# A hybrid encoder step: down-weight differences nine steps behind their fetches, their stores fourteen

## The chip, the cores and the metric

The kernel runs on one core of one Trainium2 chip, in one launch. The metric is the device time in microseconds, the median of several runs. TensorE is PE below, VectorE DVE, ScalarE ACT, GpSimd POOL; SP is the engine whose queue issues most transfers.

## The reference, cut to what matters

One layer, width 1024, float32, over a prompt of 2048 rows and a sample of 8 x 16 rows:

```python
h = rms_norm(x); z = h @ w_in
A = chunk_band_attention(z)            # 8 heads x 64, own chunk of 64 + 8 before, relative bias
B = mlstm(z)                           # 4 heads x 128, exp input gate, running-max stabiliser
x = x + rms_norm(concat(rms_norm(A), sigmoid(o) * head_rms_norm(B)) @ w_out)
u = rms_norm(x) @ w_up                 # 2 x 2816 columns
y = causal_conv_width_3(u)
x = x + rms_norm((gelu(gate) * up) @ w_down)
```

What the change touches is `w_down` alone. The kernel multiplies by it with fast products in which blocks of `w_down` are combined beforehand by subtraction; those combinations are called differences here, and they depend on the weights only.

## The kernel before, in words

Until about 1000 us of the span the kernel is in its mixers. The input projection runs as 14 groups of columns (`GROUPS`: va, qk, qb, vo) for each of two halves of the rows. Every float32 product is made as three passes over a high and a low part (`mm3`, lines 100 to 102), so each weight tile `wi{i}_raw` is split by ACT (`wi_h`) and DVE (`wi_l`). Beside each unit of the projection `pump` takes steps of two pipes, one of attention heads (`s`, `tmp`, `mn`, `pt`) and one of mLSTM heads (masks `mb`, decay weights `w`, `ms`, `ma`, `num`, state `cst`), by a budget of PE and DVE costs. The sample's attention reads cached keys (`skr`) and values (`svr`) and a bias (`nbs`). The projection's results leave through staging tiles (`qk_st`) to DRAM and are fetched again by the heads (`qraw`, `kraw`, `vraw`). Then come the output projection and the conv FFN in three blocks of rows.

The FFN needs four differences of `w_down`'s blocks. The generator `folds` makes them ahead, during the mixers, in 22 pieces (11 row groups `k`, two column halves `c`). A piece is a fetch of 128x4x256 floats (512 KB) by SP into one of three buffers, four subtracts of 128x256 on DVE in place (line 1182), and a store by SP to `wtd[k]` in DRAM (line 1202). `next(fold)` takes one step of it in each unit of the groups 2 to 12, and the rest runs out at the end of the last group. `FOLD_STEPS` is 12, so a new piece is fetched every 12 steps. In the code before, the subtracts are emitted 3 steps behind the fetch and the store 5 steps behind it. `wtd` is first read in the FFN, at 1733 us.

The whole program is recorded first. A scheduler with a model of the engines then sets each engine's order, from the recorded order, the dependences and its own times; the fetches and stores of the pieces are kept in program order among themselves. So the number of steps says where a piece is recorded, not where it runs. A transfer on SP or ACT is counted on one of eight completion counters in turn, and an issue waits for the earlier transfer on its counter.

Of the kernel before, what the change touches and what calls it, by code (L numbers as in the profile page):

```python
# [10 lines left out]
F32 = mybir.dt.float32  # L11
F32R = mybir.dt.float32r
AF = mybir.ActivationFunctionType
ALU = mybir.AluOpType
# [3 lines left out]
P = 128  # L18
D = 1024
# [21 lines left out]
NK = NF // 2  # L41
FOLD_STEPS = 12
# [7 lines left out]
def hymba_step(ctx: ExitStack, tc: tile.TileContext, I: dict, O: dict):  # L50
    nc = tc.nc
# [7 lines left out]
    def ps_mm(name):  # L59
        return psum.tile([P, 512], F32, tag="mm", name=name)  # L60

    def ps_big(name):
        return psum.tile([P, 1024], F32, tag="big", name=name)

    def ps_sm(name):
        return psum.tile([P, 512], F32, tag="sm", name=name)

    def dt_(shape, name):
        return dram.tile(shape, F32, tag=name, name=name)
# [51 lines left out]
    wtd = [dt_([P, 2048], f"wtd{k}") for k in range(NK)]  # L121
# [12 lines left out]
    pr = p1.enter_context(tc.tile_pool(name="pr", bufs=1))  # L134
# [1024 lines left out]
            nc.scalar.copy(hi, lo.bitcast(F32))  # L1159
            nc.vector.tensor_tensor(lo, lo.bitcast(F32), hi, op=ALU.subtract)  # L1160

    def fold_pieces():

        for k in range(NK):
            for c in range(2):
                yield f"d{k}_{c}", I["w_down"][k], wtd[k], c, True

    def folds():

        v4 = lambda t: t.rearrange("p (a n) -> p a n", a=4)  # L1170
        live = deque()
        pieces = list(fold_pieces())

        def load(nm, src, dst, c, down):
            cols = slice(c * 256, (c + 1) * 256)
            t = v4(pr.tile([P, D], F32, tag="fold", name=f"fold{nm}", bufs=3))
            tc.keep_in_program_order(nc.sync.dma_start(t, v4(src)[:, :, cols]))
            live.append((t, v4(dst)[:, :, cols], down))

        def combine(t, dst, down):  # L1180
            a, b, c, d = [t[:, i] for i in range(4)]
            sub = lambda o, x, y: nc.vector.tensor_tensor(o, x, y, op=ALU.subtract)
            if down:
                sub(a, b, a)
                sub(b, c, b)
                sub(c, c, a)
                sub(d, d, c)
            else:
                sub(a, a, d)
                nc.vector.tensor_tensor(d, d, c, op=ALU.add)  # L1190
                sub(c, c, a)
                sub(b, b, c)

        for n in range(FOLD_STEPS * (len(pieces) + 1)):
            i, r = divmod(n, FOLD_STEPS)
            if r == 0 and i < len(pieces):
                load(*pieces[i])
            if (n - 3) % FOLD_STEPS == 0 and 0 <= n - 3 < FOLD_STEPS * len(pieces):
                combine(*live[-1])
            if (n - 5) % FOLD_STEPS == 0 and 0 <= n - 5 < FOLD_STEPS * len(pieces):  # L1200
                t, dst, _ = live.popleft()
                tc.keep_in_program_order(nc.sync.dma_start(dst, t))
            yield

    GROUPS = ["va0", "qk0", "qk1", "va1", "qk2", "qk3", "qb0", "vo0", "qb1", "vo1", "qb2", "vo2", "qb3", "vo3"]
# [39 lines left out]
    norms = norm_steps(0)  # L1245
    next(norms)
    fold = folds()
    pend = load_group(0)
    for _ in pend[2]:
# [3 lines left out]
    for n_, (half, gi) in enumerate(seq):  # L1253
        wh, wl, _ = pend
# [5 lines left out]
        i = int(g[2])  # L1260
        nm = f"{g}_{half}"
# [208 lines left out]
    for b, tiles in enumerate(FBLOCKS):  # L1470
        last = b == len(FBLOCKS) - 1
        nt = len(tiles)
        n = HALF[b]
# [120 lines left out]
        for fi, f in enumerate(FORDER):  # L1594
# [8 lines left out]
            nm = f"{b}_{f}"  # L1603
            a, d_, ec = ps_mm(f"ua{nm}"), ps_sm(f"ub{nm}"), ps_big(f"uec{nm}")
            e, c = ec[:, 0:512], ec[:, 512:1024]
# [46 lines left out]
        if not last:  # L1652
# [47 lines left out]
            for p, (_, _, set_, onto) in enumerate(SEQUENCE):  # L1700
                for c in range(3):
# [8 lines left out]
                    for k in range(4 * c, min(4 * c + 4, NK)):  # L1710
                        i = 6 * p + k // 2
# [189 lines left out]
```

## Time and profile before

| | us |
|---|---|
| median of 3 runs | 2814.16 (2811.02 to 2815.5) |
| the profiled execution, whole | 2809.64 |
| its span | 2807.9 |
| PE busy in the span | 2707.0 |
| DVE busy | 1971.0 |
| ACT busy | 1441.0 |
| fetches of pieces: first and last start | 67.4 and 870.2 |
| stores of pieces: first and last start | 88.0 and 913.0 |

The span runs from the first to the last recorded instruction; the execution takes 1.74 us more. Busy time of engines overlaps, so it does not add up. The clock granted to PE was 0.992 of the full one over the span.

### The profile page before, as it was taken

Reading aid. Unit: us, or ns where it says so; the run is one execution under the profiler, and the core shown is the slowest. Engines: PE = TensorE matmul, PEld = TensorE weight load, DVE = VectorE, ACT = ScalarE, POOL = GpSimd, SP = SyncE. Lnnn points to the kernel's source line nnn. Section 1 sums busy time; section 2 is a strip of 40 time slices with the busy share of each in tenths; the row PEclk is TensorE's granted clock in tenths of the full one; section 3 lists DMA queues with packets and bytes.
Section 4 is the critical chain, followed back from the end, with each engine's and each line's share of the span. In section 5 each row is a group of like instructions: output and inputs, shape, how many; then the busy total and the mean of one; then the engine's idle time right before and its main releaser. Section 6 shows DMA issues by size and latency. Waiting matters only on the chain. (4 is left out here: it accounts for less than half of the span.)

```text
span 2807.9 us, 47466 instructions
## 1 busy us (share of the span) xinstructions
PE 2707.0 (96%) x16389; PEld 2524.4 (90%) x16389; DVE 1971.0 (70%) x3685; ACT 1441.0 (51%) x2922; POOL 474.9 (17%) x895
## 2 busy tenths in 40 slices
PE   8899999999899999999999999999999999999998
PEld 7899999988799997888899997789999778999877
DVE  5355555656556667767899998668888885888855
ACT  4354444635346666543454547555455565555533
POOL 1000010212100002235222211111111221222220
PEclk9999999999999999999999999999999999999999
DMA  5645456567574555345655557675555797555585
GB/s 187 178 131 159 149 173 189 174 195 236 171 223 146 159 158 173 127 147 183 232 185 170 194 173 263 201 242 163 174 176 162 273 309 240 173 177 178 184 311 185
DMA packets 359888, 535.12 MB, mean 191 GB/s; under 512 B 58882, under 2 KB 198110, under 8 KB 359518
## 3 DMA queue, kind: packets, MB, share of 16 engines
q1 hardware_dynamic: 319134, 491.95, 55.2%
q10 hardware_dynamic: 38592, 33.83, 3.6%
q0 software_dynamic: 1920, 6.29, 0.6%
q8 instruction: 129, 2.11, 0.3%
q14 instruction: 113, 0.93, 0.1%
HBM read 383.87 MB, written 151.21 MB: 191 GB/s over the span
## 5 line engine op out<-in xcount | busy, mean ns | idle before, releaser
L100 PE MATMUL uec<-B,wuh 128*128 128x384 f32 (+1 forms) x720 | 236.7, 330 | 10.8 <-DVE uu L1633 7.4
L101 PE MATMUL uec<-B,wuh 128*128 128x384 f32 (+1 forms) x720 | 235.5, 327 | 0.0
L102 PE MATMUL uec<-B,wul 128*128 128x384 f32 (+1 forms) x720 | 234.2, 327 | 0.0
L1322 ACT CAST wuh<-wu 128x512 fp32r<-128x512 f32 x255 | 141.8, 618 | 84.1 <-PE uec L101 79.5
L1323 DVE TENSOR_TENSOR wul<-wu,wuh 128x512 fp32r<-128x512 f32 x255 | 165.3, 685 | 15.3 <-ACT wuh L1322 11.7
L100 PE MATMUL vo<-wi_h,hT 128*128 128x256 f32 x544 | 157.4, 289 | 2.3 <-DVE mt L207 2.3
L102 PE MATMUL vo<-wi_h,hT 128*128 128x256 f32 x544 | 156.7, 288 | 0.0
L101 PE MATMUL vo<-wi_l,hT 128*128 128x256 f32 x544 | 156.4, 288 | 0.0
L100 PEld LDWEIGHTS uec<-B,wuh 128*128 128x128 f32 x720 | 135.4, 188 | 16.7 <-DVE uu L1633 10.0
L1323 DVE TENSOR_TENSOR wdl<-wdr,wdh 128x512 fp32r<-128x512 f32 x198 | 130.1, 700 | 27.1 <-ACT wdh L1322 27.1
L401 DVE CUSTOM_DVE_ANT_0 tmp<-s,nb 128x640 f32<-128x640 f32 (+4 forms) x128 | 94.2, 737 | 73.3 <-PE s L391 72.8
L402 ACT ACTIVATE tmp<-tmp,mn 128x640 f32<-128x640 f32 (+4 forms) x128 | 97.7, 763 | 84.1 <-DVE mn L401 82.8
L100 PE MATMUL qk<-hT,wi_h 128*128 128x384 f32 (+1 forms) x384 | 130.1, 339 | 7.8 <-ACT qk_st L234 4.3
L101 PEld LDWEIGHTS uec<-B,wuh 128*128 128x128 f32 x720 | 135.6, 188 | 0.2
L102 PEld LDWEIGHTS uec<-B,wul 128*128 128x128 f32 x720 | 135.4, 188 | 0.0
L1322 ACT CAST wdh<-wdr 128x512 fp32r<-128x512 f32 x198 | 111.7, 617 | 44.0 <-DMA wdr<-in_w_down 16.7
L414 DVE TENSOR_TENSOR ptl<-pt,pth 128x640 fp32r<-128x640 f32 (+4 forms) x128 | 93.8, 737 | 54.2 <-ACT pth L413 53.5
L102 PE MATMUL qk<-hT,wi_l 128*128 128x384 f32 (+1 forms) x384 | 129.9, 338 | 0.0
L100 PE MATMUL dn<-wdh,ah 128*128 128x512 f32 x308 | 122.8, 399 | 6.8 <-ACT wdh L1322 6.2
L101 PE MATMUL qk<-hT,wi_h 128*128 128x384 f32 (+1 forms) x384 | 128.7, 335 | 0.0
L101 PE MATMUL qb<-hT,wi_h 128*128 128x384 f32 (+1 forms) x384 | 128.3, 334 | 0.0
L100 PE MATMUL qb<-hT,wi_h 128*128 128x384 f32 (+1 forms) x384 | 127.6, 332 | 0.0
(445 smaller groups left out, 9144.8 us busy)
## 6 DMA issues: line engine op xcount, KB each, us to landing
wu<-in_w_up SPq DMA_DIRECT2D x220, 256.0 KB, 4.0
wu<-wsd SPq DMA_DIRECT2D x176, 256.0 KB, 3.9
wdr<-in_w_down SPq DMA_DIRECT2D x110, 256.0 KB, 5.4
wi_raw<-in_w_in SPq DMA_DIRECT2D x52, 512.0 KB, 4.5
wsd<-ws SPq DMA_DIRECT2D x88, 256.0 KB, 2.5
wdr<-wtd SPq DMA_DIRECT2D x88, 256.0 KB, 6.0
ad_S<-g SPq DMA_DIRECT2D x88, 192.0 KB, 2.0
ar<-ad_S SPq DMA_DIRECT2D x40, 384.0 KB, 4.8
```

The source lines that it names most:

```text
L100: nc.tensor.matmul(out, ah, bh, start=start, stop=False, skip_group_check=onto)
L101: nc.tensor.matmul(out, ah, bl, start=False, stop=False, skip_group_check=onto)
L102: nc.tensor.matmul(out, al, bh, start=False, stop=stop, skip_group_check=onto)
L401: nc.vector.tensor_tensor_reduce(o_, s_, b_, 1.0, 3e38, ALU.add, ALU.min, accum_out=mn)
L402: nc.scalar.activation(tmp[:, :n], tmp[:, :n], AF.Exp, bias=mn, scale=-1.0, accum_out=rsum[:, i % 4, hh:hh + 1])
L414: nc.vector.tensor_tensor(s.ptl[:, sl, qc], ptv, s.pth[:, sl, qc], op=ALU.subtract)
L1322: nc.scalar.copy(h, r)
L1323: nc.vector.tensor_tensor(l, r, h, op=ALU.subtract)
```

## The change

The subtracts of a piece are recorded nine steps behind its fetch instead of three, and its store five steps behind that, 14 steps behind the fetch instead of five; with 12 steps between fetches a store is now recorded after the next piece's fetch. A branch for another kind of piece, which was never taken, and the generator that listed the pieces are gone, and the tile is named `fold` instead of `foldd`. The subtracts are now on line 1176, the stores on line 1180, and every later line has a number that is 16 lower.

```diff
...
-        for n in range(FOLD_STEPS * (len(pieces) + 1)):
-            i, r = divmod(n, FOLD_STEPS)
-            if r == 0 and i < len(pieces):
-                load(*pieces[i])
-            if (n - 3) % FOLD_STEPS == 0 and 0 <= n - 3 < FOLD_STEPS * len(pieces):
-                combine(*live[-1])
-            if (n - 5) % FOLD_STEPS == 0 and 0 <= n - 5 < FOLD_STEPS * len(pieces):
-                t, dst, _ = live.popleft()
-                tc.keep_in_program_order(nc.sync.dma_start(dst, t))
...
+        def load(i):
+            k, c = pieces[i]
+            live[i] = v4(pr.tile([P, D], F32, tag="fold", name=f"fold{k}_{c}", bufs=3))
+            tc.keep_in_program_order(nc.sync.dma_start(live[i], v4(I["w_down"][k])[:, :, c * 256:(c + 1) * 256]))
+
+        def combine(i):
+            a, b, c, d = [live[i][:, x] for x in range(4)]
+            for o, x, y in ((a, b, a), (b, c, b), (c, c, a), (d, d, c)):
+                nc.vector.tensor_tensor(o, x, y, op=ALU.subtract)
+
+        def store(i):
+            k, c = pieces[i]
+            tc.keep_in_program_order(nc.sync.dma_start(v4(wtd[k])[:, :, c * 256:(c + 1) * 256], live.pop(i)))
+
+        for n in range(FOLD_STEPS * (len(pieces) + 2)):
+            for lag, do in ((0, load), (9, combine), (14, store)):
+                i, r = divmod(n - lag, FOLD_STEPS)
+                if r == 0 and 0 <= i < len(pieces):
+                    do(i)
             yield
```

The numbers of instructions of each engine stay as they were. In what follows, `foldK_C` (`folddK_C` before) is the piece of row group K and column half C, `wtdK<-` its store, and the number at the end of a name a running one.

On SP at the start of the mixers, where key halves (`kraw`) of the first heads, the first decay tables (`md`, `dd`, `dec`) and the first mask (`mb0_0`) are transferred, the order before was:

```order
L1202 DMA wtd0_240<-foldd0_0_1163 512x1x256
L345 DMA kraw1_0_0_1323<-kTd0_0_78 64x512
L590 DMA md0_1117<-cm0_1046 32x128
L591 DMA dd0_1118<-pk0_1108 32x1
L345 DMA kraw1_0_0_1323<-kTd0_0_78 64x512
L359 DMA vraw1_0_0_1355<-vd0_0_114 128x4x64
L593 DMA dec0_1121<-dd0_1118 128x32
L310 DMA relrow_310<-ext_934 128x767 x2
L1220 DMA wi4_raw0_1434<-in_w_in1 128x1024
L1177 DMA foldd0_1_1436<-in_w_down 128x4x256
```

and it is now:

```order
L345 DMA kraw1_0_0_1318<-kTd0_0_78 64x512 x2
L590 DMA md0_1117<-cm0_1046 32x128
L591 DMA dd0_1118<-pk0_1108 32x1
L359 DMA vraw1_0_0_1354<-vd0_0_114 128x4x64
L593 DMA dec0_1121<-dd0_1118 128x32
L310 DMA relrow_310<-ext_934 128x767 x2
L1204 DMA wi4_raw0_1433<-in_w_in1 128x1024
L1171 DMA fold0_1_1435<-in_w_down 128x4x256
L342 DMA qraw0_1_1473<-qTd0_1_95 64x512 x2
L345 DMA kraw0_1_0_1474<-kTd0_0_78 64x512 x2
L345 DMA kraw0_1_1_1475<-kTd0_1_79 64x512 x2
L1180 DMA wtd0_240<-fold0_0_1163 512x1x256
```

The first store has gone from ahead of the two `kraw1_0_0` halves to a place behind `kraw0_1_1`, directly ahead of the mask, which before followed `kraw0_1_1` at once, and the halves are no longer parted by the tables.

On SP around the fetch of piece 3_1, where the sample's cached keys (`skr0`), an attention result (`mixd0`), a weight tile (`wi10_raw1`) and the sample's bias (`nbs0`) are transferred, before:

```order
L1177 DMA foldd3_0_3740<-in_w_down 128x4x256
L855 DMA skr0_0_3762<-in_cache_k 128x512
L855 DMA skr0_1_3781<-in_cache_k 128x512
L1177 DMA foldd3_1_4048<-in_w_down 128x4x256
L448 DMA mixd0_162<-attst2_0_3327 512x1x128
L1202 DMA wtd2_242<-foldd2_1_3309 512x1x256
L1220 DMA wi10_raw1_4705<-in_w_in1 128x1024
L1177 DMA foldd4_0_4533<-in_w_down 128x4x256
L838 DMA nbs0_3705<-relrow_310 16x528 x8
```

and now:

```order
L1171 DMA fold3_0_3739<-in_w_down 128x4x256
L855 DMA skr0_0_3761<-in_cache_k 128x512
L855 DMA skr0_1_3781<-in_cache_k 128x512
L1180 DMA wtd2_242<-fold2_1_3308 512x1x256
L1171 DMA fold3_1_4047<-in_w_down 128x4x256
L448 DMA mixd0_162<-attst2_0_3326 512x1x128
L1180 DMA wtd2_242<-fold2_0_2855 512x1x256
L1204 DMA wi10_raw1_4701<-in_w_in1 128x1024
L1171 DMA fold4_0_4532<-in_w_down 128x4x256
L838 DMA nbs0_3704<-relrow_310 16x528 x8
```

The store of 2_1 has moved from behind the fetch of 3_1 to ahead of it, and the store of 2_0, which stood 17 rows higher up, now stands ahead of the fetch of 4_0. With three buffers, each of the two fetches takes the one that the store just ahead of it frees.

On DVE around the subtracts of piece 7_0, where the mLSTM's decay weights (`w2`), state (`cst2`) and numerators (`num2`) of one head are made, before:

```order
L1182 TENSOR_TENSOR foldd7_0_8344<-foldd7_0_8344 128x256 x2
L709 SCALAR_TENSOR_TENSOR cst2_325<-cst2_325,dec0_1121,ma2_2_1_6527 128x129
L1182 TENSOR_TENSOR foldd7_0_8344<-foldd7_0_8344 128x256
L700 TENSOR_TENSOR w2_4_0_6554<-ms2_4_0_6551,w2_4_0_6554 128x128
L1182 TENSOR_TENSOR foldd7_0_8344<-foldd7_0_8344 128x256
L657 SCALAR_TENSOR_TENSOR mvo2_4_6475<-mvo2_4_6475,hgm2_0_6318 128x2x128
L712 TENSOR_TENSOR num2_2_6505<-num2_2_6505,ma2_2_1_6527 128x129
L646 SCALAR_TENSOR_TENSOR ad2_2_6559<-num2_2_6505 128x2
```

and now:

```order
L657 SCALAR_TENSOR_TENSOR mvo2_4_6470<-mvo2_4_6470,hgm2_0_6318 128x2x128
L709 SCALAR_TENSOR_TENSOR cst2_325<-cst2_325,dec0_1121,ma2_2_1_6526 128x129
L700 TENSOR_TENSOR w2_4_0_6553<-ms2_4_0_6550,w2_4_0_6553 128x128
L1176 TENSOR_TENSOR fold7_0_8343<-fold7_0_8343 128x256
L712 TENSOR_TENSOR num2_2_6500<-num2_2_6500,ma2_2_1_6526 128x129
L1176 TENSOR_TENSOR fold7_0_8343<-fold7_0_8343 128x256
L646 SCALAR_TENSOR_TENSOR ad2_2_6558<-num2_2_6500 128x2
L1176 TENSOR_TENSOR fold7_0_8343<-fold7_0_8343 128x256
```

The group of four subtracts is spread, and `mvo2_4`, the state's update and `w2_4_0` have moved from between or behind the subtracts to ahead of the first.

Further on SP, the store of 8_1 stood directly ahead of `dec1` and of the masks `mb0_8`, `mb0_10` and `mb0_12`. Now it comes 15 rows later, the store of 8_0 stands among the value fetches `svr6` just before, and `dec1` comes behind the first two of these masks. On ACT the weights `w0_8_0` and `w0_8_1` now come ahead of the copy `qk3_1_st1_1`, behind which they stood. In the FFN, PE's order differs at the end of the first block of rows.

More of the change, by code (lines that the diff above doesn't have):

```diff
@@ L1160, in late_B @@
             nc.vector.tensor_tensor(lo, lo.bitcast(F32), hi, op=ALU.subtract)
[L1162 to L1166, printed above, removed]
     def folds():
         v4 = lambda t: t.rearrange("p (a n) -> p a n", a=4)
[L1171 to L1192, printed above, removed]
-        for n in range(FOLD_STEPS * (len(pieces) + 1)):
-            i, r = divmod(n, FOLD_STEPS)
-            if r == 0 and i < len(pieces):
-                load(*pieces[i])
-            if (n - 3) % FOLD_STEPS == 0 and 0 <= n - 3 < FOLD_STEPS * len(pieces):
-                combine(*live[-1])
-            if (n - 5) % FOLD_STEPS == 0 and 0 <= n - 5 < FOLD_STEPS * len(pieces):
-                t, dst, _ = live.popleft()
-                tc.keep_in_program_order(nc.sync.dma_start(dst, t))
@@ new lines, in folds @@
+        pieces = [(k, c) for k in range(NK) for c in range(2)]
+        live = {}
+        def load(i):
[6 more added lines that the diff above has]
+                nc.vector.tensor_tensor(o, x, y, op=ALU.subtract)
```

## The prediction

> **What bounds the kernel now.** I read the busy time first, then the span cut by stage, then the waits of TensorE (PE), then those of VectorE (DVE), and last single stretches of the timeline. The page gives each engine's busy time, its share of the span and its instruction count:
>
> ```profile
> PE 2707.0 (96%) x16389; PEld 2524.4 (90%) x16389; DVE 1971.0 (70%) x3685; ACT 1441.0 (51%) x2922; POOL 474.9 (17%) x895
> ```
>
> PE is busy for 96% of the span. The change leaves every computation in place, so it can only win or lose time in which PE stands still or runs slowly. The fetches, differences and stores of the pieces lie between 67 and 913 us. The windows over that part and the rest (stretch, length, then busy us and instruction count of PE, PEld, DVE, ACT and POOL, then the clock granted to PE, DMA share, GB/s):
>
> ```profile
> 60.00:200.00 140.00, 131.63 (x852) 128.26 (x851) 60.52 (x157) 58.31 (x133) 2.34 (x11) 0.96 0.57 168
> 200.00:330.00 130.00, 130.00 (x906) 129.21 (x905) 68.63 (x153) 64.72 (x150) 0.69 (x5) 1.00 0.48 147
> 330.00:560.00 230.00, 224.37 (x1672) 218.87 (x1671) 134.30 (x319) 123.54 (x297) 26.86 (x76) 0.99 0.58 178
> 560.00:700.00 140.00, 130.56 (x910) 123.78 (x910) 80.71 (x256) 57.82 (x165) 25.88 (x75) 1.00 0.69 215
> 700.00:800.00 100.00, 91.95 (x551) 83.41 (x550) 49.49 (x135) 37.83 (x90) 13.11 (x37) 0.97 0.60 181
> 800.00:920.00 120.00, 118.55 (x909) 116.52 (x908) 74.75 (x162) 72.26 (x167) 3.38 (x12) 1.00 0.61 182
> ```
>
> PE idles 8.4, 0.0, 5.6, 9.4, 8.1 and 1.5 us in these six stretches, 33 us together. Beside that stands the time lost to a lower clock. That is the whole purse. The list of DVE's waits and the row of the differences' group (line 1182: instructions, busy us, mean ns, idle before them) say what the change aims at:
>
> ```profile
> DVE foldd L1182 <- DMA foldd<-in_w_down: 47.1, 20, 9.8
> DVE foldd L1182 <- DMA nbs<-relrow: 2.2, 1, 2.2
> L1182 DVE TENSOR_TENSOR foldd<-foldd 128x256 f32<-128x256 f32 x88 | 36.9, 421 | 50.6 <-DMA foldd<-in_w_down 47.1 <-DMA nbs<-relrow 2.2
> ```
>
> DVE stands 47.1 us in 20 of the 22 pieces until the piece has landed, and everything that follows in its order stands with it. But PE's own list of waits in 60 to 930 us (us, times, longest) names no piece, and its largest rows are small:
>
> ```profile
> PE cus L789 <- DMA cs<-in_state_c: 4.8, 5, 1.9
> PE qk L100 <- ACT qk_st L234: 4.3, 2, 2.7
> PE sot L100 <- ACT sph L898: 3.8, 1, 3.8
> PE qk L100 <- ACT qk_st L232: 2.8, 1, 2.8
> ```
>
> Most of the 47.1 us is idle time of an engine that was ahead of PE anyway: in 200 to 330 us DVE waited for five pieces, and PE was busy for 130.00 of 130 us.
>
> **The change part by part.** *Differences nine steps behind.* No instruction is added or removed. The step at which the generator emits four subtracts moves, but a scheduler writes DVE's order. Counted in the built programs, the first subtract of 13 of the 22 pieces has just as many other DVE instructions ahead of it as before; the others move by one to five, only that of piece 4_1 by ten. So on DVE the program hardly gets the distance that the lag names, and I expect the wait row at 35 to 55 us again, 45 in the middle (47.1 less the two waits below that do change). Cost of this part by itself: nothing where the order stands. What hides it is PE's lead over DVE in the rows above; where a subtract moved, the places below price it.
>
> *Stores five steps behind that.* Of the 22 stores 21 move later, by 2 to 72 rows of SP's order; that of piece 2_1 moves 4 rows ahead. Their data is read in the FFN, so nothing waits for the values. What counts is what each is moved past, and whether a fetch needs its buffer. I take four places that PE's waits or the order single out.
>
> *Start, 90 to 119 us.* The store of piece 0_0 no longer stands ahead of the two key halves, and the halves go out together. ACT, PE and DVE rows (start, length, in brackets the idle time ahead and what ended it):
>
> ```profile
> 98.75 0.62 ACT L354 CAST kh<-kraw 128x512 fp32r<-128x512 f32 x1 [5.01 <-DMA kraw<-kTd]
> 99.81 0.44 PE L100 MATMUL qk<-hT,wi_h 128*128 128x384 f32 x1 [1.64 <-ACT qk_st L234]
> 110.41 1.80 DVE L1182 TENSOR_TENSOR foldd<-foldd 128x256 f32<-128x256 f32 x4 [9.79 <-DMA foldd<-in_w_down]
> 111.38 0.69 PE L100 MATMUL qk<-hT,wi_h 128*128 128x384 f32 x1 [2.83 <-ACT qk_st L232]
> 115.25 0.46 ACT L232 COPY qk_st<-qk 128x384 f32<-128x384 f32 x1
> 118.75 0.28 PE L100 MATMUL va<-wi_h,hT 128*128 128x256 f32 x1
> ```
>
> ACT waited 5.01 us for keys while PE's next accumulator waited for ACT, 1.64 us; earlier keys remove that. The 2.83 us at 111.38 can go the same way. What is late next is the copy at 115.25, which frees an accumulator for the group that starts at 118.75. It stands behind the decay weights, whose mask fetch mb0_0 is now behind one more store on SP (an issue takes about 0.6 us). With that copy about 0.6 to 1.1 us later, the new group can't start before about 116.8. I take −2.0 for the place: between −6 (1.64 + 2.83, and part of a half-clock stretch, below) and +1 (the copy's delay alone).
>
> *Fetch of piece 3_1, 316 to 342 us.* In the new order the store of 2_1 stands directly ahead of this fetch, which takes that buffer, and the store of 2_0 directly ahead of the next. SP, DVE and PE:
>
> ```profile
> 315.79 1.81 DVE L1182 TENSOR_TENSOR foldd<-foldd 128x256 f32<-128x256 f32 x4 [1.46 <-DMA foldd<-in_w_down]
> 316.22 0.55 SPq L1177 DMA_DIRECT2D foldd<-in_w_down  x1
> 323.21 1.35 DVE L1182 TENSOR_TENSOR foldd<-foldd 128x256 f32<-128x256 f32 x3 [0.90 <-DMA foldd<-in_w_down]
> 325.79 0.42 DVE L1182 TENSOR_TENSOR foldd<-foldd 128x256 f32<-128x256 f32 x1
> 329.32 0.65 SPq L1202 DMA_DIRECT2D wtd<-foldd  x1
> 333.10 0.59 SPq L1177 DMA_DIRECT2D foldd<-in_w_down  x1
> 333.79 5.49 SPq L838 DMA_DIRECT2D nbs<-relrow  x8
> 341.35 0.77 PE L72 MATMUL pt<-ident,tmp 128*128 128x128 f32 x5 [1.33 <-DVE mn L401]
> DMA to landing us min/median/max: 3.8/5.5/9.8
> ```
>
> The last row is the tile's issue-to-landing time, fetches and stores together. Piece 2_1's differences end at 317.6 (315.79 + 1.81), so its store can go then and lands some 4 to 7 us later. The fetch therefore moves from 316.2 to 321.5–325, and its data lands at 327–334 rather than 323.2. The old order had one such pair, and there it cost 3.8 us of SP time (329.32 to 333.10); the new one has two. The mask fetch, then store 2_0, the next fetch and the eight nbs fetches (old end 339.3) follow some 3 us later. Behind the stalled subtracts on DVE stand a weight split and the attention's tmp and mn, whose last link PE awaits at 341.35. DVE has slack of a few us between. I take +2.5 (0 if the slack covers it, +4 if not).
>
> *Place of the DVE wait at 616 us.*
>
> ```profile
> 616.56 0.88 DVE L1182 TENSOR_TENSOR foldd<-foldd 128x256 f32<-128x256 f32 x2 [5.64 <-DMA foldd<-in_w_down]
> 617.96 0.28 DVE L700 TENSOR_TENSOR w<-ms,w 128x128 f32<-128x128 f32 x1
> 618.29 0.49 PE L694 MATMUL ms<-mqk 128*128 128x128 f32 x2 [1.50 <-DVE w L700]
> ```
>
> Here the piece does hold PE: w stands behind three subtracts and PE waits for it. The new DVE order puts the mLSTM's work ahead of them. −1.5 (0 to −2).
>
> *Mask fetch at 758 to 770 us.* SP's store of 8_1 stood ahead of the mask fetches; the new order has it some 15 issues later, and the weights w ahead of an ACT copy that stood before them.
>
> ```profile
> 761.43 7.36 SPq L672 DMA_DIRECT2D mb<-md  x3
> 767.67 0.40 ACT L697 ACTIVATE w<-mb,colsp 128x128 f32<-128x128 f32 x1 [7.73 <-POOL mb L681]
> 769.07 0.58 ACT L898 CAST sph<-spt 128x512 fp32r<-128x512 f32 x1 [0.70 <-issue]
> 769.70 0.79 PE L100 MATMUL sot<-svh,sph 128*128 128x512 f32 x1 [3.83 <-ACT sph L898]
> ```
>
> ACT's queue waited 7.73 us for the mask, sph stands behind w, and PE waited 3.83 us for sph. Without the store and with dec1's transfer behind it, the first mask fetch can go some 3 us earlier (761.4 to about 758.5). I take −2.0 (0 to −3.8, PE's whole wait).
>
> *Elsewhere.* The completion counters that the transfers share are dealt out anew, so small parts of every engine's order shift; PE's order changes even in the FFN's first block, long after the last store. The row over the rest of the span:
>
> ```profile
> 1000.00:2807.90 1807.90, 1752.43 (x9639) 1598.30 (x9638) 1416.32 (x2312) 947.12 (x1748) 386.81 (x626) 0.99 0.61 199
> ```
>
> PE idles 55.5 us there, 3%, in many small pieces. A shuffle may take or give a few of them: 0, ends −4 and +4.
>
> *Half clock.* Each loss of some us in PE can cost more than itself. Windows around three of the stops above and one more:
>
> ```profile
> 110.50:117.30 6.80, 5.92 (x19) 5.92 (x20) 2.32 (x7) 2.11 (x7) 0.78 (x2) 0.50 0.40 122
> 431.40:438.20 6.80, 6.38 (x30) 6.38 (x31) 5.06 (x14) 3.11 (x9) 0.00 (x0) 0.50 0.70 216
> 769.30:772.70 3.40, 3.00 (x8) 2.61 (x9) 2.24 (x5) 2.42 (x6) 0.41 (x1) 0.50 0.53 169
> ```
>
> PE was granted half its clock there, for 3.4 or 6.8 us at a time, around stops of 2.83 and 3.83 us and, at 431 us, with only 0.4 us of idle time inside. Such a stretch costs 1.5 to 3.2 us of work (half of the busy 3.00 to 6.38). It is in the outer ends above and not in my values. The Trainium skill, TensorE: Matmul & The Clock Gate, section "What's actually happening", has half rate only after an idle window of about 3.4 us. By that rule a stop of 2.83 us costs 2.83 us alone: the start's outer end would be −4.5, and the sum's outer end 1.5 us less far. The trace does not agree, since the 2.83 us stop stands in a half-rate stretch; I go by the rows.
>
> **The sum.** −2.0 + 2.5 − 1.5 − 2.0 + 0 = −3.0 us. The profiled execution took 2809.64 us (a span of 2807.9 and 1.74 around it), 4.5 us under the median of 2814.16. I take the difference over to the median: 2814.16 − 3.0 = 2811. A change under 0.2%, 5.6 us, is about what a measurement of this kernel cannot tell from none.
>
> **The rivals.** *Faster: the fetch waits do hold PE up.* All places come out at their good ends, −6 + 0 − 2 − 3.8 = −11.8: 2802. For it: at 618 and at 341 us PE's wait ends on a DVE result with subtracts ahead of it. Against it: DVE's order, in which 13 pieces have not moved, and PE's list of waits, where no piece appears.
>
> *Slower: the fetch that now waits for a store.* The place is 316 to 342 us. If the store of 2_1 takes 7 us and the fetch behind it up to the 9.8 us of the tile's row, its data lands near 335. DVE, which by its order is free for it at about 326 (the old fourth subtract, behind nearly the same work, started at 325.79), stands for over 8 us, with the attention's tmp and the split of the next weights behind it. DVE's slack up to 341 us takes some 2 us; PE then stands for 6 us and gets a half-rate stretch of 6.8 us, 3.4 us lost: +9.4, and with the start's −2.0 and nothing from the others 2814.16 + 7.4 = 2822. It decides once the data lands more than about 3 us after DVE is ready, at 329 to 330. For it: the old trace's one such pair cost SP 3.8 us. Against it: 130.00 busy us of 130 just before, so PE has work of its own while DVE stands.
>
> *The stores crowd the fetches.* The DMA engines are busy for 0.60 of the window 700 to 800 us, and at about 700 us the new order puts two stores of 512 KB among the sample's key and value fetches. Two transfers that give up 2.5 us each turn the sum into +2.0: 2816. The Trainium skill, DMA: Bandwidth & Descriptors, section "Issuing engines are not separate DMA queues", says that transfers from all queues run on the same 16 engines and interleave. By it the stores cost their neighbours time wherever they stand; the page row of shares agrees that there is little more than a third left free, and no run here shows the slowing.
>
> *It does not do what it says.* If the order of DVE is all that counts and the four places cancel, nothing happens: 2814.
>
> **How the numbers follow.** The forecast, small terms of both signs, gets 0.48 with a range of its own of 2804 to 2818; the fetch waits that hold PE 0.22; the fetch behind the store 0.20; crowding 0.05; nothing 0.05. In the forecast case about 0.3 lies below 2808.5 and about 0.06 above 2819.8. Faster by over 0.2%: 0.48 × 0.3 + 0.22 = 0.36. Slower: 0.48 × 0.06 + 0.20 + 0.03 of the tails = 0.26. Within 0.2%: 0.38. The range of 2797 to 2824 holds both main rivals with a few us around them; what lies outside is one in ten at each end, good ends together with FFN's −4 below, and the slower rival with FFN's +4 above.
>
> **What would show it.** Right: the DVE wait for pieces is again 35 to 55 us; PE's wait for qk_st falls from 7.1 us to under 5 us; the wait for sph at 770 us falls below 2 us; the fetch of piece 3_1 starts after 321 us. Wrong: the DVE wait falls under 20 us and PE's idle time in 60 to 930 us by over 8 us (the first rival), PE idles for several us between 326 and 345 us (the second), or the time moves by over 6 us with PE's idle time in 60 to 930 us unchanged, in which case the shuffle in the FFN, which I put at nothing, made it.

## The result and the profile after

The changed kernel takes 2807.16 us (median of 12 runs, 2800.64 to 2812.28), the kernel before 2816.0 (12 runs, 2810.55 to 2823.01). The ratio of the runs is 0.9965, with a 95% interval of 0.9955 to 0.9976: 0.35% or 9.9 us less. The two medians alone lie 8.8 us apart.

The two profiled executions do not show it. The one of before took 2809.64 us, less than any of these twelve runs; the one of the change was the longest of its runs (2812.28), and their spans are 2807.9 and 2810.6 us. So the comparison below goes by stretches between fixed marks in PE's work, over thirteen profiles, and not by one pair of spans. The profiled execution of `sub3_store5` took 6807 us, where its other runs took about 2811, and is left out. The first row is from the page of the changed kernel, the next from the list of DVE's waits in 60 to 930 us, the rest from that of PE's:

```profile
PE 2711.0 (96%) x16389; PEld 2531.9 (90%) x16389; DVE 1971.9 (70%) x3685; ACT 1441.5 (51%) x2922; POOL 473.1 (17%) x895
...
DVE fold L1176 <- DMA fold<-in_w_down: 46.2, 17, 10.9
...
PE qk L100 <- ACT qk_st L234: 5.2, 2, 3.0
PE pt L72 <- ACT tmp L402: 4.5, 3, 3.4
PE cus L789 <- DMA cs<-in_state_c: 3.7, 3, 1.4
PE va L100 <- ACT qk_st L232: 3.3, 1, 3.3
PE ms L694 <- DVE w L700: 3.3, 1, 3.3
...
PE qk L100 <- ACT qk_st L232: 2.7, 1, 2.7
```

DVE waits for pieces as long as before: 46.2 us instead of 47.1. PE's wait of 3.8 us for `sph` has left the list. The `qk` matmuls wait 7.9 us for `qk_st` (5.2 and 2.7) where it was 7.1, and the `va` matmuls, which did not wait before, wait 3.3 us for it too. The wait for the decay weights `w` is 3.3 us at 710 us, where it was 1.5 us at 618.

The marks are the first-pass matmuls (line 100) of the projections, counted by tile: the 1st, 137th, 201st, 301st and 501st `vo` (256, 361, 442, 805 and 1034 us before) and the first matmul of the output projection (1069 us). All thirteen profiles have the projection matmuls in one order, and PE does the same number of matmuls in each stretch to within two (`no_subtracts` six fewer in the last). The stretch from the 501st `vo` to the output projection is called the end of the mixers. One more, from the 337th `qk` to the 209th `qb` (724 to 779 us before), holds the mask fetch and the sample's attention around it. Four windows, before and after: 724 to 779, 442 to 805, 805 to the output projection, and the end of the mixers, which is the last part of the third.

```profile
724.20:779.00 54.80, 50.12 (x283) 45.30 (x282) 26.56 (x73) 19.65 (x43) 6.51 (x22) 0.94 0.54 163
442.10:805.40 363.30, 343.94 (x2396) 326.86 (x2395) 209.45 (x563) 167.22 (x420) 57.47 (x159) 0.99 0.63 194
805.40:1069.30 263.90, 258.77 (x2013) 256.27 (x2012) 168.07 (x390) 166.20 (x398) 15.23 (x48) 0.99 0.56 167
1033.60:1069.30 35.70, 32.03 (x259) 31.34 (x257) 24.21 (x54) 24.78 (x57) 1.68 (x6) 0.95 0.54 165
```

```profile
732.00:780.80 48.80, 46.81 (x283) 42.95 (x282) 25.69 (x70) 19.69 (x44) 6.34 (x18) 1.00 0.57 177
443.10:808.60 365.50, 343.55 (x2393) 327.22 (x2392) 211.06 (x569) 168.47 (x419) 55.33 (x159) 0.99 0.64 195
808.60:1073.90 265.30, 259.82 (x2012) 257.10 (x2011) 166.45 (x387) 164.45 (x397) 15.53 (x47) 0.99 0.56 166
1041.90:1073.90 32.00, 30.73 (x257) 29.91 (x256) 23.53 (x51) 24.83 (x57) 1.71 (x5) 1.00 0.58 171
```

The stretch of 724 to 779 us is 6.0 us shorter, and PE has its whole clock there. The end of the mixers is 3.7 us shorter, also at the whole clock; but the stretch ahead of it is 5 us longer, so that from the 301st `vo` to the output projection nothing is won (265.3 us, before 263.9). The FFN is the same: from the output projection to the end it took 1738.7 us before, and 1732 to 1739 in all the other profiles.

The stretches of all kernels, in us, read off the starts of the marks in each trace (ratio with its interval; the column of 724 to 779 is a part of the one ahead of it):

| kernel | ratio | 256-361 | 361-442 | 442-805 | 724-779 | 805-1034 | end of mixers |
|---|---|---|---|---|---|---|---|
| before | 1 | 105.1 | 80.9 | 363.3 | 54.8 | 228.2 | 35.7 |
| last_three_stores14 | 0.9999 (0.9987-1.0011) | 105.0 | 78.1 | 368.5 | 55.4 | 229.2 | 36.6 |
| only_store_8_1 | 1.0003 (0.9995-1.0012) | 104.2 | 77.4 | 368.5 | 53.6 | 227.7 | 36.9 |
| early_stores14 | 1.0001 (0.9990-1.0013) | 108.1 | 75.1 | 373.9 | 56.9 | 229.4 | 36.0 |
| no_subtracts | 0.9994 (0.9984-1.0004) | 103.8 | 76.7 | 371.5 | 58.2 | 230.4 | 32.1 |
| sub3_store11 | 1.0032 (1.0021-1.0043) | 105.6 | 78.0 | 367.9 | 49.5 | 230.0 | 37.6 |
| sub3_store20 | 1.0012 (1.0003-1.0022) | 106.0 | 81.9 | 369.0 | 50.3 | 230.5 | 36.3 |
| late_but_8_1 | 0.9987 (0.9976-0.9999) | 106.0 | 78.6 | 359.7 | 47.4 | 228.4 | 37.7 |
| late_stores14 | 0.9968 (0.9957-0.9979) | 104.6 | 78.0 | 363.0 | 49.2 | 232.7 | 33.1 |
| first_two_and_late | 0.9972 (0.9963-0.9981) | 105.5 | 76.5 | 361.9 | 47.3 | 234.1 | 32.7 |
| change_but_2_0_2_1 | 0.9967 (0.9955-0.9978) | 106.0 | 76.4 | 361.1 | 47.3 | 232.8 | 32.5 |
| sub3_store14 | 0.9961 (0.9947-0.9974) | 106.0 | 75.4 | 361.1 | 48.3 | 232.2 | 32.0 |
| the change | 0.9965 (0.9955-0.9976) | 108.6 | 75.3 | 365.5 | 48.8 | 233.2 | 32.1 |

The profiles are single executions: the last two rows are one and the same program, and their spans are 2796.7 and 2810.6 us. Only what a whole group of rows shares can be read from this table. The last six rows, with the late stores at 14 steps (one of them without that of 8_1), have spans that are 9.2 us shorter on average than the other seven. Of that, 6.8 us lie in 442 to 805 us (362.1 against 368.9 on average), 1.0 ahead of it and 1.7 in the FFN, where the two groups overlap, and none between 805 us and the output projection (265.5 against 265.2).

### The profile page after: what moved, and what is told of

The parts are those of the page before. It is cut to its first block, busy times and chain, and to the rows that moved or that the text cites. A ratio compares the mean times of both kernels' runs of the same rounds, so it can differ in the third digit from the quotient of the medians.

```text
span 2810.6 us, 47450 instructions
## 1 busy us (share of the span) xinstructions
PE 2711.0 (96%) x16389; PEld 2531.9 (90%) x16389; DVE 1971.9 (70%) x3685; ACT 1441.5 (51%) x2922; POOL 473.1 (17%) x895
## 4 chain that ended last, share of the span: by engine, by line
PE 64%; DMA 15%; DVE 10%; issue 4%; ACT 4%; POOL 1%; SPq 1%; DVEq 0%; ACTq 0%; POOLq 0%
PE uec L100 4%; PE uec L101 4%; PE uec L102 4%; PE dn L101 3%; PE dn L102 3%; PE dn L100 3%; DMA wu<-in_w_up 2%; PE ua L102 2%; PE ua L100 2%; PE ua L101 2%; PE qb L100 2%; PE qb L101 2%; PE qb L102 2%; PE dnm L102 2%; DMA fold<-in_w_down 2%
## 5 line engine op out<-in xcount | busy, mean ns | idle before, releaser
L100 PE MATMUL qb<-hT,wi_h 128*128 128x384 f32 (+1 forms) x384 | 127.0, 331 | 1.2 <-ACT qk_st L232 1.2
L102 PE MATMUL qb<-hT,wi_l 128*128 128x384 f32 (+1 forms) x384 | 127.3, 331 | 0.0
```

What stands on the lines that cost most here:

```text
L100: nc.tensor.matmul(out, ah, bh, start=start, stop=False, skip_group_check=onto)
L102: nc.tensor.matmul(out, al, bh, start=False, stop=stop, skip_group_check=onto)
```

## The experiments

The first theory is that only the stores' step acts, and that it acts through the order that the scheduler writes (with places where PE's stops come and go); its rivals are that the subtracts' distance pays, or the stores' distance itself.

All times are against the kernel before in five rounds on the same chip. A diff shows the changed lines of the changed kernel's `folds`.

### Which half of the edit acts

The subtracts were put back to three steps, the stores left at fourteen:

```diff
-            for lag, do in ((0, load), (9, combine), (14, store)):
+            for lag, do in ((0, load), (3, combine), (14, store)):
```

> The subtracts are put back to three steps behind the fetch, the stores stay at 14. Built, this gives the changed kernel's program instruction for instruction. Theory A (only the stores' step acts): ratio to the kernel before 0.9965 as for the change, within 0.9945 to 0.9985. Rival (the subtracts' distance gives the gain): 1.000.

Measured: 2804.93 us, ratio 0.9961 (0.9947 to 0.9974). The half of the edit that gives it its name does nothing. With the subtracts 3, 6, 8, 9 or 10 steps behind the fetch and the stores 14, the built program is the same, row for row, on all five engines; of these, 3 and 9 were run. Only the stores' step acts. Why is not shown: the transfers of the pieces are asked to keep their recorded order and the subtracts are not, but that order is not kept strictly either. Before, the store of 2_1, recorded at step 65, goes out behind the fetches of 3_0 and 3_1, recorded at steps 72 and 84.

With (3, combine), (5, store) in the new form:

> Both steps as before, in the new form of the code; built, it is the program of before. Every theory: ratio 1.000 within 0.002. Its profile is a second look at the kernel before, whose first profiled execution was its fastest: I expect a span of 2811 to 2818 us, and a granted clock below 0.992 if the clock makes the difference between executions.

Measured: 2811.43 us, ratio 0.9998 (0.9986 to 1.0010). The new form of the code is free. Its trace has the order of before on PE, DVE and SP. For the stretches, `last_three_stores14`, below, stands in for a second profile of before: on PE and DVE it has the order of before as well, and it shows how far two executions can differ (368.5 and 363.3 us in 442 to 805).

### Is it the distance

(3, combine) with (11, store), and with (20, store):

> Stores 11 steps behind the fetch instead of 5 or 14. If the distance itself pays (stores out of the way of what follows the fetch), it lies between before and the change: ratio 0.997 to 0.999. If the order that the scheduler happens to write decides, anything from 0.994 to 1.005, and nearness to 14 says nothing.

> Stores 20 steps behind the fetch, past the next piece's subtracts. If the distance pays, at least as fast as the change: ratio 0.994 to 0.997, unless the third buffer now holds fetches back, which would show as fetches waiting for stores on SP (two such waits, 7.3 us, in the changed kernel's profile) and as 1.000 to 1.004. If the written order decides, anything from 0.994 to 1.005.

Measured: 2822.53 us, ratio 1.0032 (1.0021 to 1.0043), and 2816.45 us, ratio 1.0012 (1.0003 to 1.0022). Five steps give 1, eleven 1.0032, fourteen 0.9961 and 0.9965, twenty 1.0012. There is no trend, so the distance is not what pays. Nor does the third buffer hold fetches back at twenty steps: in that trace no fetch of a piece waits for a store, while two do in the change's (7.3 us together). Each step makes the scheduler write another order of all engines (the stores at 4 to 18, 20 and 23 steps give seventeen different programs when built), and that the order decides is what is left. Both kernels have the short stretch of 724 to 779 us (49.5 and 50.3), but lose more in the rest of 442 to 805, which takes 318.4 and 318.7 us in them and 308.5 to 317.0 in the others. At the end of the mixers both have the order of before, and both the half clock; that of eleven steps:

```profile
1041.20:1078.80 37.60, 33.60 (x259) 32.70 (x257) 24.20 (x54) 24.93 (x57) 1.68 (x6) 0.91 0.53 159
```

### Which stores

One step for some pieces and another for the rest; the condition is `i < 10`, `i >= 10` or `i >= 19`:

```diff
-            for lag, do in ((0, load), (9, combine), (14, store)):
+            for lag, do in ((0, load), (3, combine), (5, store), (14, store)):
                 i, r = divmod(n - lag, FOLD_STEPS)
-                if r == 0 and 0 <= i < len(pieces):
+                if r == 0 and 0 <= i < len(pieces) and (do is not store or lag == (14 if i < 10 else 5)):
```

> Stores of the first ten pieces 14 steps behind their fetch, the other twelve 5. Built, SP's order around the heads' fetches at 420 to 440 us is that of the change, and PE's order at the end of the mixers (1034 to 1069 us) that of before. Theory (the gain is made at these two places, 5.5 and 3.8 us): the stretch from 361 to 442 us takes 75 to 76 us instead of 80.9, the one at the end of the mixers 35 to 37 as before, ratio 0.998 (0.997 to 0.999). Rival (the gain is spread over the mixers, and the distance of the stores makes it): ten of 22 stores give ten twenty-seconds, 0.9983, with both stretches between before and the change.

> The other half: the first ten stores 5 steps behind, the last twelve 14. Built, SP's order at 420 to 440 us is that of before and PE's order at the end of the mixers that of the change. Theory: 80 to 82 us in the stretch from 361 to 442, 31.5 to 32.5 us at the end of the mixers instead of 35.7, ratio 0.9985 (0.9975 to 0.9995). Rival (spread, by distance): 0.998, with both stretches in between.

> Only the last three stores 14 steps behind. Built, the orders of PE and DVE are those of before, and only these stores stand elsewhere on SP. Theory (what the stores' place does to the orders of the others is what counts): 1.000 within 0.0015, with 80 to 82 us in the stretch from 361 to 442 us and 35 to 37 at the end of the mixers. Rival (a store's own place on the queue and the DMA engines pays): 0.9995 or less, by three twenty-seconds of 0.0035.

Measured: early 2811.62 us, 1.0001 (0.9990 to 1.0013); late 2803.48 us, 0.9968 (0.9957 to 0.9979); last three 2811.52 us, 0.9999 (0.9987 to 1.0011). The late half has the whole gain, where both theories gave each half a share. Windows of 442 to 805 us and of the end of the mixers, of the early half, the late half and the last three in this order:

```profile
439.80:813.70 373.90, 347.77 (x2393) 330.24 (x2392) 210.99 (x569) 167.74 (x420) 57.28 (x159) 0.98 0.62 191
1043.10:1079.10 36.00, 32.30 (x259) 31.61 (x257) 24.23 (x54) 24.93 (x57) 1.68 (x6) 0.95 0.53 162
```

```profile
439.00:802.00 363.00, 341.85 (x2395) 324.87 (x2394) 210.91 (x567) 169.04 (x422) 54.12 (x159) 1.00 0.64 195
1034.70:1067.80 33.10, 31.22 (x259) 30.08 (x257) 23.30 (x51) 24.35 (x57) 1.55 (x5) 1.00 0.55 165
```

```profile
440.90:809.40 368.50, 346.10 (x2393) 328.80 (x2394) 209.87 (x566) 167.44 (x421) 55.23 (x159) 0.99 0.63 192
1038.60:1075.10 36.50, 32.98 (x257) 32.29 (x256) 24.13 (x53) 24.73 (x57) 1.68 (x6) 0.91 0.53 162
```

The late half has the end of the mixers at 33.1 us and full clock, the other two have it as before. In 361 to 442 us the early half is 3 to 6 us faster than the last three and before (75.1, 78.1 and 80.9), as expected, but it has given that back by 1034 us (3 us more in 256 to 361, and 5 to 11 more in 442 to 805). So my theory was right about how the two stretches would come out, and wrong about what they are worth. The 5.5 us at 361 to 442 us are no gain. Nor are the 3 to 4 us at the end of the mixers: the late half takes 232.7 us in the stretch ahead of it, the last three 229.2 and before 228.2, so from the 301st `vo` to the output projection the three take 265.7, 265.7 and 263.9 us. What the late half wins over the other two lies in 442 to 805 us (363.0 against 368.5 and 373.9), and most of it in 724 to 779 (49.2 against 55.4 and 56.9). Before's own profile has 363.3 us in the longer stretch, but 54.8 in the shorter one.

### Is DVE's wait for pieces worth anything

The subtracts left out of the kernel with the steps of before:

```diff
-            for lag, do in ((0, load), (9, combine), (14, store)):
+            for lag, do in ((0, load), (5, store)):
```

> The steps of before with the 88 subtracts left out (the pieces are stored as they were fetched, so the FFN multiplies by other blocks). DVE loses 37 us of work and its 47 us of waiting for pieces. Theory (that wait is DVE's lead over PE and costs nothing): 0.997 to 1.003, the scatter that a newly written order gives, and PE's idle time in the mixers within 5 us of before. Rival (the wait holds PE up, 8 to 12 us): 0.9955 or less.

Measured: 2810.89 us, ratio 0.9994 (0.9984 to 1.0004). Taking 37 us of work and 47 us of waiting from DVE gives 1.7 us at best guess and 4.5 us at most, so the rival's 8 to 12 us are not there. One doubt stays: without the subtracts the scheduler wrote the rest anew too, and a new order alone has moved the time by up to 0.4% in these runs, so a small gain and a worse order could hide each other. The windows of 442 to 805 us and of the end of the mixers:

```profile
438.20:809.70 371.50, 348.33 (x2395) 331.27 (x2394) 196.55 (x529) 169.61 (x421) 53.30 (x159) 0.98 0.62 191
1040.10:1072.30 32.20, 30.30 (x253) 29.47 (x251) 22.23 (x49) 23.31 (x54) 1.39 (x4) 1.00 0.53 153
```

### The store of 8_1, alone and left behind

The condition is `i == 17`, then `i >= 10 and i != 17`:

> Only the store of piece 8_1 is 14 steps behind its fetch, the other 21 stores 5. Built, it differs from before by two rows on SP, one on ACT, four on PE and none on DVE: the store stands behind the mask fetches mb0_8 to mb0_12, and the weights w0_8 ahead of the copy qk3_1_st1_1. Theory (mask fetch): PE's wait of about 3.8 us for sph near 770 us is gone and the stretch from 613 to 805 us is shorter by 4 to 5 us, as no half-clock stretch follows: ratio 0.9982 to 0.9988. Rival (the late half's gain lies in many places): the sph wait stays above 2 us or the time within 0.9993 to 1.0007.

> The last twelve stores 14 steps behind except that of 8_1, which stays at 5. Built, the order on SP and ACT around the masks is that of before, and PE's order at the end of the mixers too. Theory: the sph wait near 770 us is back at 3.5 to 4.2 us, the end of the mixers takes 35 to 37 us, and of the late half's gain (0.9968) little is left: 0.9985 to 1.000. Rival (the gain is spread over the twelve): eleven twelfths of it stay, 0.997.

Measured: alone 2812.9 us, 1.0003 (0.9995 to 1.0012); left behind 2808.17 us, 0.9987 (0.9976 to 0.9999). Alone it does to the place all that the order promised. SP, ACT and PE rows:

```profile
759.88 0.38 SPq L672 DMA_DIRECT2D mb<-md  x1
...
764.96 0.69 ACT L697 ACTIVATE w<-mb,colsp 128x128 f32<-128x128 f32 x2 [3.90 <-POOL mb L681]
765.56 0.46 ACT L232 COPY qk_st<-qk 128x384 f32<-128x384 f32 x1
...
766.07 0.44 PE L100 MATMUL qb<-hT,wi_h 128*128 128x384 f32 x1 [2.06 <-ACT qk_st L232]
```

The mask is fetched earlier, `w` stands ahead of the copy, and PE's wait for `sph` is gone. In its place PE waits 2.06 us for the copy that now stands behind `w`, because the next group needs the accumulator that it empties, and a half-clock stretch of 3.4 us follows (from 767.4 us). The stretch of 724 to 779 us takes 53.6 us and the time is that of before: the store of 8_1 alone is not worth the 4 to 5 us that were expected.

Left behind, the gain shrinks from 0.9968 to 0.9987, by 0.0019 or 5.3 us, but not by its own place: the wait for `sph` was 0.26 us and not the 3.5 to 4.2 expected. One SP row of before, then SP and PE rows of `late_but_8_1`:

```profile
760.99 0.34 SPq L593 DMA_DIRECT2D dec<-dd  x1
...
754.09 0.56 SPq L1180 DMA_DIRECT2D wtd<-fold  x1
755.43 0.38 SPq L672 DMA_DIRECT2D mb<-md  x1
759.66 0.34 SPq L593 DMA_DIRECT2D dec<-dd  x1
...
763.13 0.50 PE L100 MATMUL sot<-svh,sph 128*128 128x512 f32 x1 [0.26 <-ACT sph L898]
```

A store still stands ahead of the first mask, but the mask is fetched 4.2 us ahead of `dec`, where before it was fetched behind it (761.43 us). So the order around the masks was not that of before, as expected, and the mask can go early without moving the store of 8_1. The windows of 724 to 779 us, of 805 to the output projection and of the end of the mixers:

```profile
723.70:771.10 47.40, 46.84 (x283) 42.80 (x282) 25.17 (x69) 18.80 (x42) 7.04 (x18) 1.00 0.61 190
800.50:1066.60 266.10, 259.46 (x2014) 257.22 (x2012) 168.07 (x390) 164.67 (x398) 15.04 (x48) 0.99 0.56 165
1028.90:1066.60 37.70, 33.32 (x259) 32.47 (x257) 24.20 (x54) 24.80 (x57) 1.69 (x6) 0.91 0.54 155
```

PE's order at the end of the mixers goes back to that of before, and with it the clock; but from the 301st `vo` on this kernel takes as long as the late half (266.1 and 265.7 us). Its profiled execution (2804.95 us) is 3.2 us under its median and shows no place where the 5.3 us are lost; that stays open.

### The start and the fetch of 3_1

The condition is `i not in (4, 5)`, then `i < 2 or i >= 10`:

> The change with the stores of 2_0 and 2_1 put back to 5 steps. Built, SP's order around the fetch of piece 3_1 is that of before (the fetch ahead of the store of 2_1), while the masks and the end of the mixers stand as in the change. Theory (the fetch behind the store costs about 2.7 us, the price the change pays there): the stretch from the first vo matmul at 256 us to 361 us takes 105 us as before instead of 106 to 108.6, ratio 0.9950 to 0.9960, the fastest of all. Rival (that wait is covered): 0.9965 as the change.

> The stores of 0_0 and 0_1 and the last twelve 14 steps behind, the eight between 5. Theory (the start gives 1.5 us beside the late half's gain): the first projection group after the keys starts 1.5 to 2.5 us sooner, ratio 0.9958 to 0.9966. Rival (what the start gives is taken up by later waits): 0.9968 as the late half alone.

Measured: 2803.01 us, 0.9967 (0.9955 to 0.9978), and 2804.78 us, 0.9972 (0.9963 to 0.9981). Neither differs from the change (0.9965) or from the late half alone (0.9968), so both theories fail: the stretch from 256 to 361 us took 106.0 us and not 105, and the first projection group after the keys started 71.5 us after the first `qk` matmul, not sooner than before (71.0). The price at 3_1 and the gain at the start are both within what these runs can tell, and no version beats the change clear of noise.

### What the end of the mixers shows

Seven of the thirteen profiles have PE's order of before there and took 35.7 to 37.7 us at a granted clock of 0.91 to 0.95; the five with the order of the change took 32.0 to 33.1 at 1.00. `no_subtracts` has a third order and took 32.1 at 1.00. PE's rows of before:

```profile
1057.80 0.31 PE L391 MATMUL s<-kl,qs 128*128 128x320 f32 x1
1059.38 0.66 PE L72 MATMUL mT_pt<-ident,mr 128*128 128x128 f32 x4 [1.28 <-ACT vo_st L232]
...
1063.37 0.58 PE L100 MATMUL vo<-wi_h,hT 128*128 128x256 f32 x1 [2.25 <-DVE mt L207]
1063.75 0.41 PE L101 MATMUL vo<-wi_l,hT 128*128 128x256 f32 x1
1063.96 0.41 PE L102 MATMUL vo<-wi_h,hT 128*128 128x256 f32 x1
```

and of the change's program (`sub3_store14`):

```profile
1056.12 0.66 PE L72 MATMUL mT_pt<-ident,mr 128*128 128x128 f32 x4 [0.47 <-ACT vo_st L232]
...
1056.73 0.28 PE L101 MATMUL vo<-wi_l,hT 128*128 128x256 f32 x1
1056.85 0.28 PE L102 MATMUL vo<-wi_h,hT 128*128 128x256 f32 x1
...
1058.50 0.39 PE L706 MATMUL ma<-cst,mqk 128*128 128x129 f32 x2
```

Before, all 24 matmuls of the projection's last tile but one stand ahead of the first transposes of the output projection's input (`mT0_pt0`), and the mixers' last steps, `mT0_pt1` and the last tile follow. PE comes to `mT0_pt1` and to the last tile with nothing else to do, stops for 1.28 and 2.25 us, and runs at half clock behind it: the `vo` matmuls start every 0.21 us instead of 0.12. (`late_but_8_1` has one stop of 4.2 us in place of the two.) In the new order 12 of these 24 matmuls stand behind `mT0_pt0`, and six matmuls of the mLSTM (`ma`) stand inside the last tile instead of ahead of it. ACT and DVE get their time: the first stop shrinks to 0.47 us, the second is gone, a new one of 0.72 us stands ahead of the last `pt`, and no half-clock stretch follows.

But the five kernels with the new order pay for it just ahead. They take 232.2 to 234.1 us from the 301st to the 501st `vo`, the eight others 227.7 to 230.5. PE stops there for 2.0 to 3.4 us for `tmp`, at 813 to 824 us, in each of the five and in none of the others at that place. The rows of `sub3_store14` and of the change:

```profile
813.07 0.77 PE L72 MATMUL pt<-ident,tmp 128*128 128x128 f32 x5 [2.28 <-ACT tmp L402]
...
824.17 1.12 PE L72 MATMUL pt<-ident,tmp 128*128 128x128 f32 x4 [3.36 <-ACT tmp L402]
```

From the 301st `vo` to the output projection the five take 264.1 to 266.7 us and the others 262.6 to 267.5. So the new order at the end of the mixers goes with the gain and does not make it.

The stretch that does separate the kernels is 724 to 779 us. PE does the same 281 matmuls in it in every kernel (275 at twenty steps). It takes 47.3 to 50.3 us in the eight kernels whose late stores have all moved (to 11, 14 or 20 steps, in one of them all but that of 8_1), and 53.6 to 58.2 in the five where none, one or three of the late stores have. PE stands idle for 0.6 to 2.9 us of it in the eight and for 4.7 to 7.7 in the five; each of the five has at least one half-clock stretch there, of the eight only that of twenty steps. Before, the stops are PE's waits for `sph` (3.83 us) and for the sample's values `svh` (0.68 us). This was found in the traces afterwards and not forecast, and each row is one profile, but all thirteen agree. Which of the late stores does it was not tried, apart from that of 8_1, which is neither enough nor needed.

Ahead of it, five of the six kernels with the late stores at 14 steps have lost PE's wait for `w` near 618 us that the prediction named; `first_two_and_late` keeps 0.73 us, and the seven others have it or one like it (0.43 to 2.73 us). A wait for `w` of 1.8 to 3.3 us, which all six have at 702 to 710 us, takes as much back.

## Why the prediction was right or wrong

The time lies inside the range, and the change is faster, as the value of 2811 against 2814 said; but the forecast was 3 us and the measurement gives 9.9, in the part to which 0.36 was given. That the time fell inside the range is in part luck: two terms of the sum came to nothing (the start and the fetch of 3_1), and one place gave three times its term.

**The subtracts stay put: right.** The expected wait of 45 us came out at 46.2. `sub3_store14` shows more than was claimed: the nine steps change no row of the program. That the wait is DVE's lead over PE is borne out by `no_subtracts`, which without it is at most 4.5 us faster.

**The start, −2.0: the mechanism seen, the gain taken back.** In the seven kernels whose first two stores are late, PE's stop at 99.81 us is gone, as worked out. In its place the first `va` of the new group (118.75 us before) waits 2.4 to 4.7 us for the `qk_st` copy that the prediction named as late next; none of the six others has that wait. The step that failed is the copy's delay, which was put at 0.6 to 1.1 us. From the first `qk` matmul to this `va` the seven took 68.4 to 71.5 us and the six 68.9 to 71.5. The sign named for being right, PE's `qk` waits for `qk_st` under 5 us, did not come: they were 7.9 us.

**The fetch of 3_1, +2.5: seen, and free.** The rows of the change (SP, then DVE):

```profile
321.41 0.57 SPq L1180 DMA_DIRECT2D wtd<-fold  x1
326.81 0.55 SPq L1171 DMA_DIRECT2D fold<-in_w_down  x1
...
333.77 0.63 SPq L1180 DMA_DIRECT2D wtd<-fold  x1
...
337.71 0.59 SPq L1171 DMA_DIRECT2D fold<-in_w_down  x1
...
330.58 1.35 DVE L1176 TENSOR_TENSOR fold<-fold 128x256 f32<-128x256 f32 x3 [2.46 <-DMA fold<-in_w_down]
```

The fetch left 5.4 us behind the store, DVE stood for 2.5 us, all as worked out. But `change_but_2_0_2_1` without it took the same time. The failed step is the last one, from DVE's stop to PE: the stop did not reach PE, within what these runs can tell. The rival built on this place falls with it.

**The wait at 616 us, −1.5: the place right.** It is gone, or down to 0.73 us, in every kernel with the late stores at 14 steps, but the sum stopped at the place; the wait for a later `w` took its place, in the change 3.25 us:

```profile
710.16 0.49 PE L694 MATMUL ms<-mqk 128*128 128x128 f32 x2 [3.25 <-DVE w L700]
```

**The mask fetch, −2.0: the place right, its term mis-sized, the store of 8_1 not the cause.** The change's rows (SP, ACT, PE):

```profile
764.72 0.91 SPq L672 DMA_DIRECT2D mb<-md  x2
...
768.38 0.69 ACT L697 ACTIVATE w<-mb,colsp 128x128 f32<-128x128 f32 x2 [3.35 <-POOL mb L681]
768.98 0.46 ACT L232 COPY qk_st<-qk 128x384 f32<-128x384 f32 x1
...
769.49 0.44 PE L100 MATMUL qb<-hT,wi_h 128*128 128x384 f32 x1 [1.18 <-ACT qk_st L232]
```

PE's 3.83 us are gone whole, as the sign that was named (under 2 us) asked, and with them both half-clock stretches that before has in 724 to 779 us. The stretch around the place is 6 us shorter in the change and 5.6 to 7.5 in the other kernels with the late stores at 14 steps, three times the −2.0 and more than the −3.8 of the outer end: the half clock was left out of the value, and PE's other stops near the place were not priced. Nor is it the store of 8_1 alone that does it. Alone its edit is worth nothing (1.0003), for the copy behind `w`, which was named in the order and not priced, is late next; and without it the stretch is as short (47.4 us).

**Elsewhere, 0: right as a sum.** The end of the mixers gave 3.7 us and the stretch ahead of it took them back. The FFN, to whose shuffle the prediction gave a change of over 6 us with PE's idle time unchanged, took 1738.7 us before and 1736.6 in the change's profile. That sign can't be read from one pair of profiles: PE's idle time in 60 to 930 us was 32.9 us before, 38.2 in the change's profile and 31.1 in that of `sub3_store14`, the same program.

**Half clock: the rows right.** At the end of the mixers half rate follows the stops in every one of the seven profiles with the old order. The Trainium skill, TensorE: Matmul & The Clock Gate, section "What's actually happening", asks for an idle window of about 3.4 us. The rows do not agree: in before the two stops are 1.28 and 2.25 us with 1.7 us of work between them, and the clock of the window fell to 0.95.

**Crowding, and "does not do what it says".** No run shows the stores slowing fetches, and none rules it out; the pieces' own fetches took 6.0 us before and 5.6 after (median, issue to landing), their stores 5.4 and 5.5. That the change does not do what it says was true of its first half and wrong of its second.

## What to carry to other kernels

Where a scheduler writes the order, a constant that says "later" is a seed: build it with neighbouring values first, look which engines' rows change at all, and judge the distance by several values, not by two. A wait that ends at PE is worth its length only if nothing stands right behind it; undo one step alone on the chip before its wait is counted. A stretch that has become shorter is a gain only if its neighbours have not become longer: add them up before a cause is named. One profile of each kernel is not enough where executions of one program differ by more than the change; compare stretches between fixed matmuls, over several profiles.

## What the runs showed of the hardware

Two executions of one program (`sub3_store14` and the change) had spans of 2796.7 and 2810.6 us and granted clocks of 0.992 and 0.989. Three thousandths of 2800 us are 8 us, so the clock accounts for more than half of the difference of 13.9 us. Stops of one to two microseconds were enough for a half-clock stretch of 3.4 us: at the end of the mixers, where two of them (once a single one of 4.2 us) stand in a row, all seven profiles with that order got it, with 0.91 to 0.95 over the window. In the traces of before and of the change the granted clock is either the whole one or half of it, nothing between.
